# First expert products: all high halves of the weights of a unit before all low halves, and another pacing of the weight splits

## Chip, core and metric

The kernel runs on one core of one Trainium2 chip. The metric is device time in microseconds (us) for one execution of the whole layer; lower is better. The time before the change is the median of three runs, 2164.36 us (2163.01 to 2168.81 us).

## What is computed

The program is one decoder layer for 1024 tokens of width 1024: a projection, two kinds of attention, an output projection, then a mixture of 32 experts of which each token uses four. Only the experts matter for this change. In the reference (cut; the router and the sorting of tokens are left out):

```python
def expert_block(args):
    xe, e = args
    gu = xe @ w_gate_up[e] + b_gate_up[e]            # 1024 -> 2048
    g = jnp.minimum(gu[:, :D_FF], SWIGLU_LIMIT)
    u = jnp.clip(gu[:, D_FF:], -SWIGLU_LIMIT, SWIGLU_LIMIT)
    act = (u + 1.0) * (g * jax.nn.sigmoid(SWIGLU_ALPHA * g))
    return act @ w_down[e] + b_down[e]               # 1024 -> 1024
```

Everything is float32, and the 32 experts have 3 x 4 MB of weights each that must be read from HBM once.

## The kernel before

The experts run one after the other, the largest and the smaller ones alternating. An expert has a fixed number of token columns C (`CAPS`: 200 down to 136 for 17 of them, with the first, and 128 down to 96 for 15).

**Chunks.** The weights of an expert arrive as twelve chunks of 1 MB, `[128, 4, 512]` in float32: eight of the first matrix (buffers `eraw`, five of them) and four of the second (`draw`, four). SP issues their DMAs (line 782).

**Splits.** A chunk of the first matrix is split in two halves (`split_half`): ScalarE writes the high part of half a chunk as fp32r into a buffer `hb` (line 796, twelve buffers of half a chunk each), and VectorE subtracts it and writes the remainder, the low part, as bf16 into `ha` (line 797, six buffers of a whole chunk). A chunk of the second matrix is used as it is.

**Units.** The first matrix is worked in four units of 512 output columns: gate, up, gate, up (`first_products`, called twice in each pass of the loop over `half`). A unit takes two chunks (the two halves `kh` of the 1024 rows that are summed over) and four PSUM banks, one for each 128 output columns `j`. For each of its 8 row blocks `k` and 4 values of `j` there are two products on TensorE: a high one (line 1167: weights `hb`, moving data `xx`, which holds the tokens' high and low parts, 2C columns and at least 256) and a low one (line 1171: weights `ha` in bf16, moving data `xb`, the tokens in bf16, C columns). That is 32 high and 32 low products. The two kinds alternate in runs: 16 high, 16 low (first chunk), then 8 high, 8 low for `j` = 0, 1 and 8 high, 8 low for `j` = 2, 3 (second chunk). Below, H16 is a run of 16 high products, L8 a run of 8 low ones, and so on.

**After a unit.** ScalarE adds the bias while it reads a bank (`tb`, line 1179), VectorE adds the other columns of the bank (line 1183 for gate, 1181 for up), and they make the activation `aa` (lines 1197, 1198, 1207, 1208). Then 64 products with the second matrix follow (line 1220, in float32; the trace has two records for each), their results go to `yT` (line 1225), and in the middle of them stand the transposes of the next expert's tokens (`stage_t`, lines 1146 to 1150). The transposes of the result (line 1237, at most 16), the weighting (line 1239, `y`) and the scatter are put off (`later(1, back)`) until the next expert has done its first chunk; they stand on TensorE between L16 and H8 of its first unit.

**Order and pacing.** From the experts on, the order on TensorE, ScalarE, VectorE and SP is the order in which the code calls them. After each chunk `done(c)` drops the chunk from `at_["open"]`, the number of half chunks that are split and not yet used (at most 12), and calls `pump(n)`, which issues the loads for which a buffer is free and up to n splits: 1 after a chunk of the first matrix, 2 after one of the second. So `open` is 12, 10, 8 and 6 at the starts of the four units, 4 after them, and 12 again after the second matrix.

Of the kernel before, what the change touches and what calls it, by code (L numbers as in the profile page):

```python
# [20 lines left out]
P = 128  # L21
# [3 lines left out]
KT = D // P  # L25
# [52 lines left out]
def hybrid_layer(ctx: ExitStack, tc: tile.TileContext, x, c_t, w_ada, b_ada_t, b_ada, norm1_t, w_in,  # L78
                 qk_g, lam_in, diff_g, w_out, norm2_g, w_router, b_router, w_gate_up, b_gate_up,
                 w_down, b_down, b_exp_t, out):  # L80
    nc = tc.nc
# [102 lines left out]
    with ExitStack() as st:  # L184
# [335 lines left out]
        with ExitStack() as so:  # L520
# [241 lines left out]
            parts, reg = {}, {0: 0}  # L762
            at_ = {"dma": 0, "split": 0, "use": 0, "open": 0}
            raws, held = {}, {"eraw": 0, "draw": 0}
# [7 lines left out]
            def kind_of(d):  # L772
                return "eraw" if d % NCH < NGU else "draw"

            def load_chunk():
                d, kind = at_["dma"], kind_of(at_["dma"])
                i, w, n, kh = CHUNKS[d]
                e = expert_of(i)
                if d % NCH == LIX and 0 < i < E - 1:
                    lists(i + 1)  # L780
                raws[d] = pools[kind][0].tile([P, 4, NC_], F32, name=kind, bufs=pools[kind][1])
                nc.sync.dma_start(raws[d], w[ds(e, 1), kh * 512:(kh + 1) * 512, n * NC_:(n + 1) * NC_]
                                  .rearrange("o (k p) n -> p (o k) n", p=P))
                held[kind] += 1
                at_["dma"] += 1

            def split_half():

                t = at_["split"]
                c, q = t // 16 * NCH + t % 16 // 2, t % 2  # L790
                raw = raws[c][:, 2 * q:2 * q + 2]
                h_ = slot(False).rearrange("p (k n) -> p k n", k=2)
                if q == 0:
                    parts[c] = [], slot(True).bitcast(BF16).rearrange("p (k n) -> p k n", k=4)
                l_ = parts[c][1][:, 2 * q:2 * q + 2]
                nc.scalar.activation(h_, raw, AF.Copy)  # L796
                nc.vector.tensor_tensor(l_, raw, h_.bitcast(F32), OP.subtract)  # L797
                parts[c][0].extend((h_[:, j], l_[:, j]) for j in range(2))
                if q:
                    raws.pop(c)  # L800
                    held["eraw"] -= 1
                at_["open"] += 1
                at_["split"] += 1

            def pump(more):

                limit = min(at_["split"] + more, E * 16)
                while True:
                    d, t = at_["dma"], at_["split"]
                    kind = kind_of(d)  # L810
                    if d < len(CHUNKS) and kind in pools and held[kind] < pools[kind][1]:
                        load_chunk()
                    elif t < limit and t // 16 * NCH + t % 16 // 2 < d and at_["open"] < NH:
                        split_half()
                    else:
                        return
# [248 lines left out]
    with ExitStack() as se:  # L1065
# [23 lines left out]
        def take():  # L1089

            c = at_["use"]
            at_["use"] += 1
            return c, parts[c][0] if kind_of(c) == "eraw" else raws[c]

        def bank():
            return ps4.tile([P, 512], F32, name="gu", bufs=8)

        todo = []

        def done(c):  # L1100

            if kind_of(c) == "eraw":
                parts.pop(c)
                at_["open"] -= 2
                pump(1)
            else:
                raws.pop(c)
                held["draw"] -= 1
                pump(2)
            for t in todo:  # L1110
                t[0] -= 1
            while todo and todo[0][0] <= 0:
                todo.pop(0)[1]()
# [38 lines left out]
        def scatter(y, sl, n):  # L1152
            nc.gpsimd.indirect_dma_start(  # L1153
                out=out, out_offset=bass.IndirectOffsetOnAxis(ap=sl.bitcast(I32)[:n, 0:1], axis=0),
                in_=y[:n], in_offset=None, compute_op=OP.add)

        def first_products(st):


            C, xx, xb = st["C"], st["xk"], st["xb"]  # L1160
            pg = [bank() for _ in range(4)]
            for kh in range(2):
                c, w = take()
                for js in ((0, 1), (2, 3)) if kh else ((0, 1, 2, 3),):
                    for j in js:
                        for k in range(4):
                            nc.tensor.matmul(pg[j][:, :max(256, 2 * C)], w[k][0][:, j * P:(j + 1) * P], xx[4 * kh + k],  # L1167
                                             start=(kh + k == 0), stop=False)
                    for j in js:
                        for k in range(4):  # L1170
                            nc.tensor.matmul(pg[j][:, C:2 * C], w[k][1][:, j * P:(j + 1) * P], xb[:, 4 * kh + k],  # L1171
                                             start=False, stop=(kh == 1 and k == 3))
                if kh == 0:
                    done(c)
            return c, pg

        def joined(dst, p, C, bias, more=0.0):
            t = ap_.tile([P, C], F32, name="tb", bufs=TB)
# [6 lines left out]
        def expert(st, between):  # L1185
            C, bc = st["C"], st["bc"]
            a = ap_.tile([P, KT, C], F32, name="aa")
            for half in range(2):
                c, pg = first_products(st)
                gts = []  # L1190
                for q in range(2):
                    gt = ap_.tile([P, 2, C], F32, name="gt", bufs=2)
                    for j in range(2):
                        f = 4 * half + 2 * q + j
                        joined(gt[:, j], pg[2 * q + j], C, bc[:, f:f + 1])
                    sg = ap_.tile([P, 2, C], F32, name="sg")
                    nc.scalar.activation(sg, gt, AF.Sigmoid, scale=1.702)  # L1197
                    nc.vector.tensor_mul(gt, gt, sg)  # L1198
                    gts.append(gt)
                done(c)  # L1200
                c, pg = first_products(st)
                for q in range(2):
                    ut = ap_.tile([P, 2, C], F32, name="ut")
                    f = 4 * half + 2 * q
                    for j in range(2):
                        joined(ut[:, j], pg[2 * q + j], C, bc[:, KT + f + j:KT + f + j + 1], 1.0)
                    nc.vector.tensor_scalar(ut, ut, 8.0, -6.0, op0=OP.min, op1=OP.max)
                    nc.vector.scalar_tensor_tensor(a[:, f:f + 2], gts[q], GATE7, ut, op0=OP.min, op1=OP.mult)
                done(c)


            pg = [bank() for _ in range(4)]
            yT = ap_.tile([P, KT, C], F32, name="yT")
            for kh in range(2):
                for n in range(2):
                    c, w = take()
                    for j in range(4):
                        p = pg[2 * n + j // 2][:, j % 2 * 256:j % 2 * 256 + C]
                        for k in range(4):
                            nc.tensor.matmul(p, w[:, k, j * P:(j + 1) * P], a[:, 4 * kh + k],  # L1220
                                             start=(kh + k + j % 2 == 0), stop=(kh == 1 and k == 3 and j % 2 == 1))
                    if kh:
                        for j in range(4):
                            f = 4 * n + j
                            nc.scalar.activation(yT[:, f], pg[2 * n + j // 2][:, j % 2 * 256:j % 2 * 256 + C], AF.Identity,  # L1225
                                                 bias=bc[:, 2 * KT + f:2 * KT + f + 1], scale=1.0)
                    done(c)
                if kh == 0:
                    between()

            def back():
                for (t0, n), sl in zip(st["blocks"], st["slots"]):
                    y = ap_.tile([P, D], F32, name="y", bufs=2)
                    for g in range(2):
                        py = bank()
                        for k in range(4):
                            nc.tensor.transpose(py[:n, k * P:(k + 1) * P], yT[:, 4 * g + k, t0:t0 + n], ident)
                        cs = slice(g * 512, (g + 1) * 512)
                        nc.vector.scalar_tensor_tensor(y[:n, cs], py[:n], sl[:n, 1:2], gate2[:n, cs],  # L1239
                                                       op0=OP.mult, op1=OP.mult)  # L1240
                    scatter(y, sl, n)
            later(1, back)
# [57 lines left out]
        st = stage_g(0)  # L1300
# [7 lines left out]
        for i in range(E):  # L1308
            nxt = stage_g(i + 1) if i + 1 < E else None
            expert(st, lambda: nxt and stage_t(nxt))  # L1310
            st = nxt
# [4 lines left out]
    with ExitStack() as sf:  # L1316
# [4 lines left out]
        with tc.For_i(0, n_over, 1) as i:  # L1321
# [44 lines left out]
            for n in range(2):  # L1366
                c = slice(n * 512, (n + 1) * 512)
# [52 lines left out]
```

## Time and profile before

| | us |
|---|---|
| median of 3 runs | 2164.36 (2163.01 to 2168.81) |
| the profiled execution | 2167.32 |
| its span in the trace | 2165.5 |
| busy in it: TensorE (PE) | 2094.8 (97%) |
| VectorE (DVE) | 1499.6 (69%) |
| ScalarE (ACT) | 1150.2 (53%) |
| experts: from the first product to the last piece of the last expert | 742.8 to about 2153 |

The profile is of one execution. An engine is busy while at least one of its instructions runs; matmuls are pipelined (the recorded duration of one is longer than the distance to the next), so for TensorE the distances between the starts of runs are read, not the durations. A timeline row has the start, the length, the engine, the source line, the names (out<-in), the shape and the count of equal instructions that follow each other. A row of waits has the engine and line that waited, for whom, the total in us, how often, and the longest.

### The profile page before, as it was taken

Reading aid. Unit: us, or ns where it says so; the run is one execution under the profiler, and the core shown is the slowest. Engines: PE = TensorE matmul, PEld = TensorE weight load, DVE = VectorE, ACT = ScalarE, POOL = GpSimd, SP = SyncE. Lnnn points to the kernel's source line nnn. Section 1 sums busy time; section 2 is a strip of 40 time slices with the busy share of each in tenths; the row PEclk is TensorE's granted clock in tenths of the full one; section 3 lists DMA queues with packets and bytes.
Section 4 is the critical chain, followed back from the end, with each engine's and each line's share of the span. In section 5 each row is a group of like instructions: output and inputs, shape, how many; then the busy total and the mean of one; then the engine's idle time right before and its main releaser. Section 6 shows DMA issues by size and latency. Waiting matters only on the chain. (4 is left out here: it accounts for less than half of the span.)

```text
span 2165.5 us, 43655 instructions
## 1 busy us (share of the span) xinstructions
PE 2094.8 (97%) x16922; PEld 1957.5 (90%) x16922; DVE 1499.6 (69%) x2946; ACT 1150.2 (53%) x2263; POOL 429.3 (20%) x444
## 2 busy tenths in 40 slices
PE   7999999999999699999999999999999999999997
PEld 6877778998777699999999999999999999999997
DVE  6587756776666876677667677776767767667763
ACT  3522224777633455566456565656556656656652
POOL 2255532111045401111011111110111101101100
PEclk9999999999999799999999999999999999999999
DMA  7267886442224598799799999989989989999882
GB/s 294 73 163 215 221 230 172 114 109 76 89 105 153 192 356 299 247 334 350 255 292 326 300 314 319 332 312 343 315 297 312 361 297 320 323 315 335 297 320 60
DMA packets 272404, 548.98 MB, mean 254 GB/s; under 512 B 30675, under 2 KB 30691, under 8 KB 272067
## 3 DMA queue, kind: packets, MB, share of 16 engines
q1 hardware_dynamic: 250323, 490.09, 65.4%
q0 software_dynamic: 21872, 56.08, 11.1%
q8 instruction: 134, 2.20, 0.4%
q14 instruction: 75, 0.61, 0.1%
HBM read 501.31 MB, written 44.77 MB: 252 GB/s over the span
## 5 line engine op out<-in xcount | busy, mean ns | idle before, releaser
L797 DVE TENSOR_TENSOR ha<-eraw,hb 128x1024 bf16<-128x1024 f32 x512 | 601.3, 1224 | 233.5 <-ACT hb L796 233.0
L1167 PE MATMUL gu<-xx,hb 128*128 128x256 f32 (+13 forms) x4096 | 641.5, 304 | 0.6 <-DVE xx L1149 0.6
L1167 PEld LDWEIGHTS gu<-xx,hb 128*128 128x128 f32 x4096 | 561.1, 190 | 1.0 <-DVE xx L1149 0.8
L796 ACT ACTIVATE hb<-eraw 128x1024 fp32r<-128x1024 f32 x512 | 506.7, 1053 | 34.1 <-DMA eraw<-in_w_gate_up_dram 34.0
L1220 PE MATMUL gu<-aa,draw 128*128 128x128 f32 (+19 forms) x4096 | 521.2, 288 | 0.0
L1220 PEld LDWEIGHTS gu<-aa,draw 128*128 128x128 f32 x4096 | 511.2, 191 | 0.6
L1171 PE MATMUL gu<-xb,ha 128*128 128x128 bf16 (+19 forms) x4096 | 316.2, 224 | 0.0
L1179 ACT ACTIVATE tb<-gu,bcol 128x128 f32<-128x128 f32 (+19 forms) x512 | 164.6, 371 | 253.8 <-PE gu L1171 225.7
L1171 PEld LDWEIGHTS <-ha 128*128 128x128 bf16 x4096 | 246.6, 98 | 28.4 <-issue 3.3
L1153 POOL DMA_INDIRECT out_dram<-y,slot x47 | 81.6, 1736 | 528.3 <-DVE y L1239 251.4
L1126 POOL DMA_INDIRECT xg<-h2d,slot x47 | 54.5, 1160 | 629.0 <-PE gu L1146 381.8
L1225 ACT ACTIVATE yT<-gu,bcol 128x128 f32<-128x128 f32 (+19 forms) x256 | 82.4, 374 | 126.6 <-PE gu L1220 126.5
L572 DVE CUSTOM_DVE_ANT_0 p<-pss,bias 128x1024 f32<-128x1024 f32 (+7 forms) x128 | 94.4, 755 | 49.5 <-ACT p L581 22.2
L606 PE MATMUL po<-vsb,pT 128*128 128x64 f32 (+1 forms) x864 | 111.1, 275 | 2.6 <-ACT pT L600 1.5
L606 PEld LDWEIGHTS po<-vsb,pT 128*128 128x128 f32 x864 | 105.6, 194 | 4.8 <-ACT pT L600 1.8
L581 ACT ACTIVATE p<-p,mn 128x1024 f32<-128x1024 f32 (+7 forms) x128 | 98.6, 773 | 12.8 <-DVE mn L572 12.1
L1197 ACT ACTIVATE sg<-gt 128x256 f32<-128x256 f32 (+19 forms) x128 | 55.8, 436 | 89.2 <-DVE gt L1183 89.2
L461 PE MATMUL pp<-wh,hb 128*128 128x512 f32 x240 | 101.7, 424 | 0.0
L1198 DVE TENSOR_TENSOR gt<-gt,sg 128x256 f32<-128x256 f32 (+19 forms) x128 | 57.4, 448 | 63.4 <-ACT sg L1197 63.4
L112 POOL TENSOR_TENSOR rrs<-vrs,nhalf 128x8 f32<-128x8 f32 (+2 forms) x48 | 66.6, 1386 | 165.3 <-DVE vrs L110 160.2
L463 PE MATMUL pp<-wl,hb 128*128 128x512 f32 x240 | 94.9, 395 | 0.0
L462 PE MATMUL pp<-wh,hb 128*128 128x512 f32 x240 | 94.8, 395 | 0.0
(265 smaller groups left out, 2623.6 us busy)
## 6 DMA issues: line engine op xcount, KB each, us to landing
eraw<-in_w_gate_up_dram SPq DMA_DIRECT2D x256, 1024.0 KB
draw<-in_w_down_dram SPq DMA_DIRECT2D x128, 1024.0 KB
wraw<-in_w_ada_dram SPq DMA_DIRECT2D x32, 512.0 KB
wraw<-in_w_in_dram SPq DMA_DIRECT2D x23, 512.0 KB
hb<-in_w_ada_dram SPq DMA_DIRECT2D x16, 512.0 KB
qd<-tt POOLq DMA_DIRECT2D x32, 256.0 KB, 4.0
kd<-tt POOLq DMA_DIRECT2D x32, 256.0 KB, 4.2
ha<-qd SPq DMA_DIRECT2D x32, 256.0 KB
```

Of the source, the lines that this page charges most:

```text
L461: nc.tensor.matmul(pp, hh[b][:, k], wh[:, kk], start=(k == 0), stop=False)
L462: nc.tensor.matmul(pp, hl[b][:, k], wh[:, kk], start=False, stop=False)
L463: nc.tensor.matmul(pp, hh[b][:, k], wl[:, kk], start=False, stop=(k == KT - 1))
L572: nc.vector.tensor_tensor_reduce(p[:, :n], pss[:, :n], bias[:, (NB - 1 - ib) * P:(NB - 1 - ib) * P + n], -1.0, 3.0e38, OP.add, OP.min, mn)
L581: nc.scalar.activation(p, p, AF.Exp, bias=self.mn[c], scale=-1.0, accum_out=self.l[:, c:c + 1])
L606: nc.tensor.matmul(self.po[:, :w], self.pT[:, k], vsb[self.br][:, k, self.h * w:(self.h + 1) * w], start=(k == 0), stop=(k == self.ib))
L796: nc.scalar.activation(h_, raw, AF.Copy)
L797: nc.vector.tensor_tensor(l_, raw, h_.bitcast(F32), OP.subtract)
L1167: nc.tensor.matmul(pg[j][:, :max(256, 2 * C)], w[k][0][:, j * P:(j + 1) * P], xx[4 * kh + k], start=(kh + k == 0), stop=False)
L1171: nc.tensor.matmul(pg[j][:, C:2 * C], w[k][1][:, j * P:(j + 1) * P], xb[:, 4 * kh + k], start=False, stop=(kh == 1 and k == 3))
L1179: nc.scalar.activation(t, p[:, C:2 * C], AF.Identity, bias=bias, scale=1.0)
L1220: nc.tensor.matmul(p, w[:, k, j * P:(j + 1) * P], a[:, 4 * kh + k], start=(kh + k + j % 2 == 0), stop=(kh == 1 and k == 3 and j % 2 == 1))
```

## The change

In a unit both chunks are taken at its start. The high products of the first chunk come first (H16), then those of the second (H16), then all 32 low products, bank by bank (L32: 8 for each `j`). Each product stays as it was; the number of instructions on every engine is the same. The first chunk is no longer handed back alone: between the two H16 stands `step()`, a `pump(1)` and the countdown of `todo` (so the result's transposes of the previous expert now stand between the two H16 of the first unit), and both chunks are handed back at the unit's end, with two splits after a gate unit and one after an up unit. After the chunks of the second matrix come 2, 1, 2 and 1 splits in place of 2, 2, 2 and 2. `open` is then 11, 10, 8 and 7 at the starts of the units (12, 11, 9 and 8 after the `step()` in them), 5 after them and 11 again after the second matrix.

```diff
--- before.py
+++ after.py
@@ -1097,16 +1097,19 @@
 
         todo = []
 
-        def done(c):
-
-            if kind_of(c) == "eraw":
-                parts.pop(c)
-                at_["open"] -= 2
-                pump(1)
-            else:
-                raws.pop(c)
-                held["draw"] -= 1
-                pump(2)
+        def done(*cs, more=1):
+
+            for c in cs:
+                if kind_of(c) == "eraw":
+                    parts.pop(c)
+                    at_["open"] -= 2
+                else:
+                    raws.pop(c)
+                    held["draw"] -= 1
+            step(more)
+
+        def step(more=1):
+            pump(more)
             for t in todo:
                 t[0] -= 1
             while todo and todo[0][0] <= 0:
@@ -1159,20 +1162,19 @@
 
             C, xx, xb = st["C"], st["xk"], st["xb"]
             pg = [bank() for _ in range(4)]
+            two = [take() for _ in range(2)]
+            w = two[0][1] + two[1][1]
             for kh in range(2):
-                c, w = take()
-                for js in ((0, 1), (2, 3)) if kh else ((0, 1, 2, 3),):
-                    for j in js:
-                        for k in range(4):
-                            nc.tensor.matmul(pg[j][:, :max(256, 2 * C)], w[k][0][:, j * P:(j + 1) * P], xx[4 * kh + k],
-                                             start=(kh + k == 0), stop=False)
-                    for j in js:
-                        for k in range(4):
-                            nc.tensor.matmul(pg[j][:, C:2 * C], w[k][1][:, j * P:(j + 1) * P], xb[:, 4 * kh + k],
-                                             start=False, stop=(kh == 1 and k == 3))
+                for j in range(4):
+                    for k in range(4 * kh, 4 * kh + 4):
+                        nc.tensor.matmul(pg[j][:, :max(256, 2 * C)], w[k][0][:, j * P:(j + 1) * P], xx[k],
+                                         start=(k == 0), stop=False)
                 if kh == 0:
-                    done(c)
-            return c, pg
+                    step()
+            for j in range(4):
+                for k in range(KT):
+                    nc.tensor.matmul(pg[j][:, C:2 * C], w[k][1][:, j * P:(j + 1) * P], xb[:, k], start=False, stop=(k == KT - 1))
+            return two[0][0], two[1][0], pg
 
         def joined(dst, p, C, bias, more=0.0):
             t = ap_.tile([P, C], F32, name="tb", bufs=TB)
@@ -1186,7 +1188,7 @@
             C, bc = st["C"], st["bc"]
             a = ap_.tile([P, KT, C], F32, name="aa")
             for half in range(2):
-                c, pg = first_products(st)
+                c, c_, pg = first_products(st)
                 gts = []
                 for q in range(2):
                     gt = ap_.tile([P, 2, C], F32, name="gt", bufs=2)
@@ -1197,8 +1199,8 @@
                     nc.scalar.activation(sg, gt, AF.Sigmoid, scale=1.702)
                     nc.vector.tensor_mul(gt, gt, sg)
                     gts.append(gt)
-                done(c)
-                c, pg = first_products(st)
+                done(c, c_, more=2)
+                c, c_, pg = first_products(st)
                 for q in range(2):
                     ut = ap_.tile([P, 2, C], F32, name="ut")
                     f = 4 * half + 2 * q
@@ -1206,7 +1208,7 @@
                         joined(ut[:, j], pg[2 * q + j], C, bc[:, KT + f + j:KT + f + j + 1], 1.0)
                     nc.vector.tensor_scalar(ut, ut, 8.0, -6.0, op0=OP.min, op1=OP.max)
                     nc.vector.scalar_tensor_tensor(a[:, f:f + 2], gts[q], GATE7, ut, op0=OP.min, op1=OP.mult)
-                done(c)
+                done(c, c_)
 
 
             pg = [bank() for _ in range(4)]
@@ -1224,7 +1226,7 @@
                             f = 4 * n + j
                             nc.scalar.activation(yT[:, f], pg[2 * n + j // 2][:, j % 2 * 256:j % 2 * 256 + C], AF.Identity,
                                                  bias=bc[:, 2 * KT + f:2 * KT + f + 1], scale=1.0)
-                    done(c)
+                    done(c, more=2 - n)
                 if kh == 0:
                     between()
 
```

TensorE, in an expert of 120 columns, its first unit and the start of its second (`hb`, `ha`: high and low weights; `yT`: the previous expert's result, turned). Before:

```order
L1167 MATMUL gu<-xx,hb 128x256 x16
L1171 LDWEIGHTS ha
L1171 MATMUL gu<-xb,ha 128x120
...
L1237 MATMUL gu<-ident,yT 128x128 x8
L1237 MATMUL gu<-ident,yT 44x128 x8
L1167 MATMUL gu<-xx,hb 128x256 x8
...
L1167 MATMUL gu<-xx,hb 128x256 x8
...
L1167 MATMUL gu<-xx,hb 128x256 x16
```

and of the changed kernel:

```order
L1170 MATMUL gu<-xx,hb 128x256 x16
L1239 MATMUL gu<-ident,yT 128x128 x8
L1239 MATMUL gu<-ident,yT 44x128 x8
L1170 MATMUL gu<-xx,hb 128x256 x16
L1176 LDWEIGHTS ha
L1176 MATMUL gu<-xb,ha 128x120
...
L1170 MATMUL gu<-xx,hb 128x256 x32
```

The low products, each a weight load and a matmul, stood behind every run of high ones (16, 8 and 8 times the pair); now 32 pairs stand behind 32 high products, and the transposes stand inside the high ones. In the second to fourth unit nothing interrupts H32.

ScalarE, the same expert, from the end of the previous expert's second matrix to the second gate unit (`hb<-eraw`: splits; `tb`, `sg`: a unit's evaluation). Before:

```order
L1225 ACTIVATE yT<-gu,bcol 128x172 x4
L796 ACTIVATE hb<-eraw 128x1024 x3
L1179 ACTIVATE tb<-gu,bcol 128x120 x2
L1197 ACTIVATE sg<-gt 128x240
L1179 ACTIVATE tb<-gu,bcol 128x120 x2
L1197 ACTIVATE sg<-gt 128x240
L796 ACTIVATE hb<-eraw 128x1024 x2
L1179 ACTIVATE tb<-gu,bcol 128x120 x4
L796 ACTIVATE hb<-eraw 128x1024 x2
```

and of the changed kernel:

```order
L1227 ACTIVATE yT<-gu,bcol 128x172 x4
L796 ACTIVATE hb<-eraw 128x1024 x2
L1181 ACTIVATE tb<-gu,bcol 128x120 x2
L1199 ACTIVATE sg<-gt 128x240
L1181 ACTIVATE tb<-gu,bcol 128x120 x2
L1199 ACTIVATE sg<-gt 128x240
L796 ACTIVATE hb<-eraw 128x1024 x3
L1181 ACTIVATE tb<-gu,bcol 128x120 x4
L796 ACTIVATE hb<-eraw 128x1024 x2
```

Between the evaluation of a gate unit and that of the up unit behind it stand three splits in place of two, and before a gate unit of a new expert two in place of three; VectorE's order has the same shift with `ha<-eraw,hb`.

## Rows read from the trace of the kernel before

**Rows 1.** Busy time of the engines, from the page: us, share, instructions.

```profile
PE 2094.8 (97%) x16922; PEld 1957.5 (90%) x16922; DVE 1499.6 (69%) x2946; ACT 1150.2 (53%) x2263; POOL 429.3 (20%) x444
```

**Rows 2.** TensorE's waits from 742.8 us to the end.

```profile
PE gu L1167 <- DVE xx L1149: 0.6, 1, 0.6
```

**Rows 3.** Busy time by window: length, PE, PEld, DVE, ACT, POOL, clock, DMA share, GB/s.

```profile
742.80:2153.00 1410.20, 1409.76 (x13056) 1376.13 (x13056) 983.85 (x1626) 814.45 (x1499) 185.13 (x202) 1.00 0.90 307
1075.00:1380.00 305.00, 305.00 (x2904) 298.25 (x2903) 218.95 (x355) 181.10 (x335) 45.87 (x46) 1.00 0.96 313
```

**Rows 4.** Timeline of TensorE, 120 columns: a whole unit, then a later start.

```profile
1516.93 2.14 PE L1167 MATMUL gu<-xx,hb 128*128 128x256 f32 x16
1518.91 1.01 PE L1171 MATMUL gu<-xb,ha 128*128 128x120 bf16 x16
1519.73 1.19 PE L1167 MATMUL gu<-xx,hb 128*128 128x256 f32 x8
1520.77 0.59 PE L1171 MATMUL gu<-xb,ha 128*128 128x120 bf16 x8
1521.17 1.19 PE L1167 MATMUL gu<-xx,hb 128*128 128x256 f32 x8
...
1522.61 2.14 PE L1167 MATMUL gu<-xx,hb 128*128 128x256 f32 x16
...
1528.30 2.14 PE L1167 MATMUL gu<-xx,hb 128*128 128x256 f32 x16
```

**Rows 5.** Timeline of TensorE, 172 columns: high runs of one unit.

```profile
1383.92 2.75 PE L1167 MATMUL gu<-xx,hb 128*128 128x344 f32 x16
...
1387.68 1.50 PE L1167 MATMUL gu<-xx,hb 128*128 128x344 f32 x8
...
1389.59 1.51 PE L1167 MATMUL gu<-xx,hb 128*128 128x344 f32 x8
...
1391.51 2.75 PE L1167 MATMUL gu<-xx,hb 128*128 128x344 f32 x16
```

**Rows 6.** Timeline of TensorE, 200 columns: starts of runs in one unit.

```profile
848.43 3.17 PE L1167 MATMUL gu<-xx,hb 128*128 128x400 f32 x16
851.44 1.55 PE L1171 MATMUL gu<-xb,ha 128*128 128x200 bf16 x16
852.76 1.71 PE L1167 MATMUL gu<-xx,hb 128*128 128x400 f32 x8
...
854.95 1.70 PE L1167 MATMUL gu<-xx,hb 128*128 128x400 f32 x8
...
857.13 3.17 PE L1167 MATMUL gu<-xx,hb 128*128 128x400 f32 x16
```

**Rows 7.** Timeline of TensorE, first unit of an expert of 120 columns.

```profile
1428.99 1.92 PE L1237 MATMUL gu<-ident,yT 128*128 128x128 f32 x16
1430.67 1.20 PE L1167 MATMUL gu<-xx,hb 128*128 128x256 f32 x8
1431.71 0.59 PE L1171 MATMUL gu<-xb,ha 128*128 128x120 bf16 x8
```

**Rows 8.** Groups from 742.8 to 2153 us: busy, mean ns, idle before.

```profile
L797 DVE TENSOR_TENSOR ha<-eraw,hb 128x1024 bf16<-128x1024 f32 x508 | 596.7, 1224 | 233.5 <-ACT hb L796 233.0 <-issue 0.5
L796 ACT ACTIVATE hb<-eraw 128x1024 fp32r<-128x1024 f32 x508 | 502.8, 1054 | 34.1 <-DMA eraw<-in_w_gate_up_dram 34.0
L1171 PEld LDWEIGHTS <-ha 128*128 128x128 bf16 x4096 | 246.6, 98 | 28.4 <-issue 3.3
```

**Rows 9.** Timeline of VectorE, 120 columns: splits, then the end of an up unit.

```profile
1520.64 2.36 DVE L797 TENSOR_TENSOR ha<-eraw,hb 128x1024 bf16<-128x1024 f32 x2 [0.54 <-ACT hb L796]
...
1525.07 0.41 DVE L1208 SCALAR_TENSOR_TENSOR aa<-gt,ut 128x240 f32<-128x240 f32 x1
```

**Rows 10.** ScalarE's waits for chunks, from 900 us on.

```profile
ACT hb L796 <- DMA eraw<-in_w_gate_up_dram: 31.8, 8, 7.4
```

**Rows 11.** The DMA queue's own waits (SP), from 850 us on.

```profile
SPq L782 <- DVE ha L797: 626.9, 159, 10.5
```

## The prediction

> **What bounds the kernel now.** I read the page's busy times first: TensorE is busy in 2094.8 us of the span [rows 1], far more than any other engine. Then its waits over the expert stage: 0.6 us in all, at the first product of the first expert [rows 2]. The window over that stage says the same: 1409.76 us busy of 1410.20, at a granted clock of 1.00, which is the full 2.4 GHz [rows 3]. So for 1410 us the time is the sum of the distances between the starts of TensorE's instructions; nothing it needs comes late. VectorE (984 us) and ScalarE (814 us) have slack in the same window, and the DMA engines are 0.90 busy. What the change does to TensorE's own stream counts directly; what it does to the others counts only where it makes TensorE wait.
>
> The third view is TensorE's timeline of a whole unit at 120 columns [rows 4], read by starts. H16 with L16 takes 1519.73 - 1516.93 = 2.80 us. A pair H8, L8 does half that work; the two pairs behind take 1521.17 - 1519.73 = 1.44 and 1522.61 - 1521.17 = 1.44 us. Half of 2.80 is 1.40. If the products alone made the time, two short pairs would last as long as the long one; they last 2.88 against 2.80, so one more pair of runs costs 0.08 us. Each pair changes the kind of product twice, high to low and back to high, and the rows can't be explained by a new chunk, since the second H8 begins with a chunk already in use and its pair is no shorter than the first. The same reading at 172 columns gives 1.91 + 1.92 - 3.76 = 0.07 [rows 5], at 200 columns 2.19 + 2.18 - 4.33 = 0.04 us [rows 6]. I call this the price of a change: 0.08 at the narrow widths, on average 0.055 at the wide ones.
>
> **The change part by part.** No instruction is added or taken away; the edits are an order and a pacing.
>
> First, the order of a unit. The second to fourth unit of an expert go from three pairs of runs to one: two changes less each, six in an expert. In the first unit the transposes of the last expert's result cut the high run, H16, transposes, H16, L32. A high run that begins behind transposes pays as much as one behind low products: H8 behind them lasts 1431.71 - 1430.67 = 1.04 us [rows 7], and H8 behind L16 lasts 1520.77 - 1519.73 = 1.04 us too [rows 4]. So this unit still has two entries into high products (its start, and behind the transposes) where it had three, and saves one change. That is seven for an expert, and eight for the first one, which has no transposes inside. Wide experts, 17 with the first: 17 x 7 + 1 = 120 changes at 0.055 us, 6.6 us. Narrow ones: 15 x 7 = 105 at 0.08 us, 8.4 us. Sum: 15.0 us.
>
> What the rows do not show is the step from a high product to a transpose, which is new (31 times). Its nearest rows are the prices of a change: from nothing to 0.08 us, so 0 to 2.5 us of loss. Nor do they exclude that the first unit saves its second change as well, 2.5 us of gain. I take neither. For the price itself the ends are 0.04 and 0.08 everywhere: 225 x 0.04 = 9.0 and 225 x 0.08 = 18.0 us. With the two unknowns on top the gain lies between 6.5 and 20.5 us.
>
> Do runs of 32 go on as runs of 16 do? In the long pair the low run takes 1519.73 - 1518.91 = 0.82 us for 16 products, 51 ns each; L8 takes 1521.17 - 1520.77 = 0.40 us, 50 ns each [rows 4]. Doubling the run did not slow it. I take 51 ns for the products 17 to 32 as well; the other end is the first rival.
>
> Second, the splits. They are spaced 16 to an expert as before, and I cost the new pacing at nothing. What hides it is the stock of halves that are already split. At the start of the fourth unit there were 6 and are now 7, of which that unit uses 4; the last of the four was issued at the end of the second unit, before as now. That is a whole unit ahead (5.68 us at 120 columns, [rows 4]), and a split lasts 1.05 us on ScalarE and 1.22 us on VectorE [rows 8]. The second chunk's high halves are now wanted behind H16 instead of H16 and L16, 0.82 us sooner; the lows of both later. No new wait for a buffer arises: the stock reaches 12 halves, in six chunks, only at the `step()` of a first unit, which is what the twelve `hb` and six `ha` hold.
>
> Third, the queue behind the splits. Between the evaluation of a gate unit and that of the up unit there are now three splits on VectorE, not two, and the up unit's reads of its banks stand behind them: 1.22 us later. At 120 columns that evaluation ended at 1525.07 + 0.41 = 1525.48 us, and the fourth unit, which takes these banks, began at 1528.30 [rows 4, 9]: 2.82 us of cover. Off it go 1.22 us and two savings of 0.16 us, and 1.3 us stay. If that cover went, TensorE would wait once for each such place, up to 32 times. The banks also become complete closer together, in the last four runs of 8 low products; the evaluation of a gate unit starts a little later, with the same cover behind it. The transposes of the result come 0.82 us sooner behind the second matrix and have one split less ahead of them on both engines.
>
> Fourth, the loads. SP's largest wait is for VectorE, that is for a free buffer, 626.9 us in 159 waits [rows 11]. So the loads follow the splits, and with the same splits in an expert they keep their place. SP issues the same loads in the same order (only the reading of the overflow count moves, nine loads back), and GpSimd's gathers and scatters stand in the same order too.
>
> So the sum is 15.0 us, all of it on the path. The profiled execution took 2167.32 us, 3 us over the median; against it the sum gives 2152.3, against the median 2164.4 - 15.0 = 2149.4 us.
>
> **The rivals.** *The low runs get too long.* Each low product needs its own weights, a load of 98 ns [rows 8], and the products follow each other at 51 ns: that works only while loads run ahead. If the lead is used up after 16 pairs, products 17 to 32 of a unit, 128 x 16 = 2048 in all, come at 98 ns: 47 ns more each at 120 columns, 96 us if all were so narrow; at 200 columns the distance is already (852.76 - 851.44) / 16 = 82 ns [rows 6], so 16 ns more, 33 us. The middle, 64 us, against a gain of 15: 2213 us. It decides from 15.0 / 2048 = 7 ns a product. Against it: no slowing between 8 and 16. The page "TensorE: Matmul & The Clock Gate" of the Trainium skill (section "Back-to-back issue gap") speaks for it: it gives about 81 ns for a sustained stream of weight loads and matmuls of 128 columns, against 56 ns for one matmul by itself. By that the late products would lose 25 ns each, an estimate of 51 us from this page's figures; runs of 16 in this trace don't agree with it, and no run here is longer. Chance 0.06.
>
> *The weights come too late.* ScalarE waited eight times for a chunk, 31.8 us in all and up to 7.4 us [rows 10], and between 1075 and 1380 us the DMA engines were 0.96 busy [rows 3]. A faster TensorE asks for the same bytes sooner. If that stretch is held to its transfers, its 7 experts lose their share of the gain, 7/32 x 15.0 = 3.3 us: 2152.7 us. If all of the stage is, nothing is left: 2164.4 us. Against it: the waits of 7.4 us never reached TensorE, and over the whole stage 0.90 would only become 0.91. Chance of a loss over 5 us: 0.08.
>
> *The change of kind is not what costs.* The price may hang on something that stays, such as the number of bank changes or the signals to ScalarE; the order would then move nothing: 2164.4 us. Two independent widths besides 120 columns show the price, so 0.05.
>
> **How the numbers follow.** My forecast has 0.80, the three rivals 0.06, 0.08 and 0.05, and 0.01 is left for something else. A measurement here can tell about 0.3% from no change, 6.5 us, so faster means under 2157.9 us. The forecast's own range, 2143.9 to 2157.9 us, lies there whole; of the late weights half does. That makes faster 0.80 + 0.04 + 0.01 = 0.85, the same 0.04 + 0.05 = 0.09, slower 0.06. The range reaches from 2144 to 2160 us, which takes in the mild half of the second rival.
>
> **What would show it.** In the changed profile a unit of 120 columns should last about 5.68 - 0.16 = 5.52 us from start to start, its H32 about 3.9 and its L32 about 1.65 us, the last 8 low products as close as the first 8. TensorE's waits should stay near 0.6 us, and its busy time should fall by the whole gain. Low products that drift apart behind the sixteenth prove the first rival; waits of TensorE for `hb`, `ha` or a bank, with ScalarE's waits for chunks grown, the second; a unit of 5.68 us the third. I am wrong if the gain comes with new waits, or if the unit shrinks and the time doesn't.

## The result, and the profile after

The changed kernel takes 2152.31 us (median of 5 runs, 2151.51 to 2153.65), the kernel before 2167.80 us on the same occasion (5 runs, 2163.01 to 2170.88). The medians are 15.5 us apart. The ratio is 0.9931 with a 95% interval of 0.9916 to 0.9945: a gain of 15.0 us, between 11.9 and 18.2. Of all executions told of here one was slow, of the kernel order_only below (4026.11 us, at a mean granted clock of 0.91 where the others had 0.99), and its ratio leaves it out. The two extra runs of the kernel before lie higher than the three known at the forecast, so its median is 3.4 us higher than the one I started from; that is why 2152.3 is reached and not 2149.4.

TensorE's waits over the experts, in the profile after, the same kind of row as in [rows 2]:

```profile
PE gu L1170 <- DVE xx L1152: 0.6, 1, 0.6
```

Nothing new makes it wait. Its window ends earlier, and the DMA engines are 0.91 busy in place of 0.90 [rows 3]:

```profile
742.80:2139.50 1396.70, 1395.95 (x13056) 1380.99 (x13056) 977.52 (x1627) 824.80 (x1499) 182.62 (x203) 1.00 0.91 310
```

The window over the stage was 1410.2 us long and is 1396.7, and TensorE's own busy time in it fell by 13.8 us, from 1409.76 to 1395.95: the whole difference is there. The timeline after, of an expert of 120 columns from its start to the second matrix (compare [rows 4, 7]):

```profile
1503.27 2.15 PE L1170 MATMUL gu<-xx,hb 128*128 128x256 f32 x16
1505.26 1.91 PE L1239 MATMUL gu<-ident,yT 128*128 128x128 f32 x16
1506.92 2.14 PE L1170 MATMUL gu<-xx,hb 128*128 128x256 f32 x16
1508.91 1.85 PE L1176 MATMUL gu<-xb,ha 128*128 128x120 bf16 x32
1510.57 4.04 PE L1170 MATMUL gu<-xx,hb 128*128 128x256 f32 x32
1514.45 1.85 PE L1176 MATMUL gu<-xb,ha 128*128 128x120 bf16 x32
1516.12 4.03 PE L1170 MATMUL gu<-xx,hb 128*128 128x256 f32 x32
1519.99 1.85 PE L1176 MATMUL gu<-xb,ha 128*128 128x120 bf16 x32
1521.66 4.03 PE L1170 MATMUL gu<-xx,hb 128*128 128x256 f32 x32
1525.53 1.85 PE L1176 MATMUL gu<-xb,ha 128*128 128x120 bf16 x32
1527.22 3.00 PE L1222 MATMUL gu<-aa,draw 128*128 128x120 f32 x25
```

A unit lasts 1516.12 - 1510.57 = 5.55 us (forecast 5.52, before 5.68), its H32 3.88 and its L32 1.67 us. L32 is 52 ns a product, as L16 was 51: the longer run does not slow down. At 172 and at 200 columns:

```profile
1378.78 5.30 PE L1170 MATMUL gu<-xx,hb 128*128 128x344 f32 x32
1383.93 2.58 PE L1176 MATMUL gu<-xb,ha 128*128 128x172 bf16 x32
1386.30 5.31 PE L1170 MATMUL gu<-xx,hb 128*128 128x344 f32 x32
...
848.43 6.10 PE L1170 MATMUL gu<-xx,hb 128*128 128x400 f32 x32
854.37 2.92 PE L1176 MATMUL gu<-xb,ha 128*128 128x200 bf16 x32
857.07 1.16 PE L1170 MATMUL gu<-xx,hb 128*128 128x400 f32 x5
```

A unit takes 7.52 and 8.64 us, before 7.59 [rows 5] and 8.70 us [rows 6].

### The profile page after: what moved, and what is told of

Its sections match the earlier page's. It is cut to its first block, busy times and chain, and to the rows that moved or that the text cites. A ratio compares the mean times of both kernels' runs of the same rounds, so it can differ in the third digit from the quotient of the medians.

```text
span 2151.8 us, 43624 instructions
## 1 busy us (share of the span) xinstructions
PE 2079.3 (97%) x16922; PEld 1960.2 (91%) x16922; DVE 1493.2 (69%) x2946; ACT 1160.6 (54%) x2263; POOL 427.0 (20%) x444
## 5 line engine op out<-in xcount | busy, mean ns | idle before, releaser
L1170 PE MATMUL gu<-xx,hb 128*128 128x256 f32 (+13 forms) x4096 | 588.0, 300 | 0.6 <-DVE xx L1152 0.6
L1170 PEld LDWEIGHTS gu<-xx,hb 128*128 128x128 f32 x4096 | 554.6, 190 | 1.0 <-DVE xx L1152 0.8
L1181 ACT ACTIVATE tb<-gu,bcol 128x128 f32<-128x128 f32 (+19 forms) x512 | 177.0, 372 | 256.7 <-PE gu L1176 188.3
L1176 PE MATMUL gu<-xb,ha 128*128 128x128 bf16 (+19 forms) x4096 | 271.6, 224 | 0.0
L1151 ACT ACTIVATE xx<-gu 128x512 fp32r<-128x512 f32 (+19 forms) x98 | 39.5, 475 | 110.6 <-PE gu L1149 110.4
L1185 DVE TENSOR_TENSOR gt<-gu,tb 128x128 f32<-128x128 f32 (+19 forms) x256 | 68.5, 296 | 39.8 <-ACT tb L1181 35.7
```

The costliest lines, as they stand in the source:

```text
L1181: nc.scalar.activation(t, p[:, C:2 * C], AF.Identity, bias=bias, scale=1.0)
```

## The experiments

My theory: the whole gain is the 225 changes of kind that are gone, at a fixed price each, and the pacing is worth nothing. The rivals: a part of the gain is the pacing's; or the price is not of the change of kind. Each kernel was timed against the kernel before on the same chip, in five rounds.

**order_only**, the changed kernel with the old amounts of splits:

```diff
-                done(c, c_, more=2)
+                done(c, c_)
...
-                    done(c, more=2 - n)
+                    done(c, more=2)
```

> TensorE's order is that of the changed kernel; the splits are paced as in the kernel before (one at each of the two hand-backs of a unit, two after each chunk of the second matrix), so the stock is 11, 9, 7 and 5 halves at the starts of the units and 3 after them. Theory (the gain is 225 changes of kind less, the pacing is worth nothing): 13 to 17 us faster than the kernel before, a unit of 120 columns 5.53 us, TensorE's waits 0.6 us. Rival (the new pacing is needed for the gain): TensorE waits for a split or a bank in the third or fourth units, and at least 5 us of the gain are missing.

Measured: 2152.24 against 2167.28 us, ratio 0.9933 (0.9920 to 0.9946), 15.0 us between the medians. TensorE waited 0.6 us, though the stock was only 5 halves at the start of the fourth unit, and a unit of 120 columns took 1431.93 - 1426.40 = 5.53 us:

```profile
1426.40 4.02 PE L1170 MATMUL gu<-xx,hb 128*128 128x256 f32 x32
1430.27 1.85 PE L1176 MATMUL gu<-xb,ha 128*128 128x120 bf16 x32
1431.93 4.03 PE L1170 MATMUL gu<-xx,hb 128*128 128x256 f32 x32
```

The order alone brings all of it.

**pacing_only**, the changed kernel with the runs of before:

```diff
-                for j in range(4):
-                    for k in range(4 * kh, 4 * kh + 4):
-                        (a high product)
+                for js in ((0, 1), (2, 3)) if kh else ((0, 1, 2, 3),):
+                    for j in js:
+                        for k in range(4 * kh, 4 * kh + 4):
+                            (a high product)
+                    for j in js:
+                        for k in range(4 * kh, 4 * kh + 4):
+                            (a low product)
                 if kh == 0:
                     step()
-            (all low products)
```

> Both chunks of a unit are handed back together and the splits are paced as in the changed kernel, but the products stand in the runs of before (16, 16, 8, 8, 8, 8). Theory (the gain is the order's alone): within 3 us of the kernel before, a unit of 120 columns 5.67 us. Rival (a part of the gain is the pacing's): faster than before by 5 us or more.

Measured: 2167.60 against 2167.28 us, ratio 1.0004 (0.9995 to 1.0012). The pacing neither gains nor costs. Summed over the starts of all units in the trace, the experts take 0.02 us more than before.

**runs_of_4** and **runs_of_1**, the kernel before with more changes:

```diff
-                for js in ((0, 1), (2, 3)) if kh else ((0, 1, 2, 3),):
+                for js in ((0,), (1,), (2,), (3,)):
```

and for runs of 1 both products in one loop over `j` and `k`.

> The kernel before with shorter runs: 4 high and 4 low products for each bank in each chunk, eight pairs of runs in a unit in place of three, 5 x 128 = 640 more changes of kind; everything else as before. Theory (each change costs 0.04 to 0.08 us, however long the runs are): 26 to 51 us slower, nearest to 640 x 0.067 = 43 us, and no new waits of TensorE. Rival (the price hangs on the end of a bank's run or on a signal, not on the change of kind): within 10 us of before. Second rival (the price grows as the runs shrink, since weight loads can be pulled ahead less): over 60 us slower.

> The kernel before with one high and one low product by turns: 32 pairs in a unit in place of three, 29 x 128 = 3712 more changes. Theory (a fixed price of 0.067 us for a change): 3712 x 0.067 = 249 us slower, 150 to 300. Rival (the price sits in the second high product of a run, which comes 200 ns behind the first; a run of one has no second): much less than 150 us slower. Second rival (a weight load that can't be pulled ahead at all, 190 ns for a high one and 98 ns for a low one): over 350 us slower.

Measured: 2207.64 against 2167.28 us, ratio 1.0188 (1.0175 to 1.0201): 40.4 us for 640 changes, 0.063 us each. And 2412.27 against 2167.28 us, 1.1132 (1.1118 to 1.1147): 245.0 us for 3712 changes, 0.066 us each. The price is about the same whether a run has 16, 8, 4 products or one (0.061 us in the traces for the changes that the order takes away), and TensorE waited 0.6 us in both. The timeline of runs_of_1 at 120 columns:

```profile
1664.84 0.36 PE L1166 MATMUL gu<-xx,hb 128*128 128x256 f32 x1
1665.05 0.23 PE L1168 MATMUL gu<-xb,ha 128*128 128x120 bf16 x1
1665.09 0.36 PE L1166 MATMUL gu<-xx,hb 128*128 128x256 f32 x1
1665.29 0.23 PE L1168 MATMUL gu<-xb,ha 128*128 128x120 bf16 x1
1665.33 0.36 PE L1166 MATMUL gu<-xx,hb 128*128 128x256 f32 x1
```

A pair takes (1665.33 - 1664.84) / 2 = 0.245 us, where a high and a low product inside long runs take 3.88 / 32 + 1.67 / 32 = 0.173 us. The recorded start of the high product is only 0.04 us behind the low one; the low one behind it starts 0.21 us later. So the lost time stands between the start of the high product and what follows it, which asks for its cause.

**cover_16** and **cover_96.** In the kernel before, the weight loads (PEld) around a return to high products stand like this:

```profile
1518.90 0.85 PEld L1171 LDWEIGHTS <-ha 128*128 128x128 bf16 x16
1519.71 1.01 PEld L1167 LDWEIGHTS gu<-xx,hb 128*128 128x128 f32 x8
```

The last low product alone, the second high load alone, and the high loads of the whole stage (times, mean ns):

```profile
1519.70 0.22 PE L1171 MATMUL gu<-xb,ha 128*128 128x120 bf16 x1
...
1519.82 0.19 PEld L1167 LDWEIGHTS gu<-xx,hb 128*128 128x128 f32 x1
...
L1167 PEld LDWEIGHTS gu<-xx,hb 128*128 128x128 f32 x4096 | 561.1, 190 | 1.0 <-DVE xx L1149 0.8
```

The first load of high weights begins at 1519.71 us, just behind the start of the last low product at 1519.70. One high load lasts 190 ns, a low one 98 ns [rows 8]. Theory: the price is that part of this load that the one product before it doesn't hide. Not all of the 190 ns can count, since 190 - 52 = 138 ns would be about twice the price; the second high load begins only 0.11 us behind the first. Then an extra, useless low product in front of the high run stands under the load, whatever its width:

```diff
+                    if (js[0] == 0 and kh) or (kh == 0 and u):
+                        nc.tensor.matmul(pg[3][:, 400:416], w[3][1][:, js[-1] * P:(js[-1] + 1) * P],
+                                         xb[:, 4 * kh + 3, :16], start=False, stop=False)
```

> The kernel before with 224 extra low products, one behind the last low product of a run wherever a high run of the same unit follows (not behind the first chunk of an expert's first unit): the same weights again, 16 columns, into an unused part of a bank. Theory (the price of going back to high products is the load of the high weights, 190 ns long, which begins with the last low product and is hidden only while that product runs): the extra product stands under the load, so each costs what the low product before it takes, 43 to 86 ns with 61 in the mean, 224 x 0.061 = 13.7 us, the same as with 96 columns. Rival (a fixed price behind the end of the low products): each costs its own distance, some 28 ns, 6 us.

> As cover_16 with 96 columns in each extra low product. Theory (the load of the high weights hides it): 13.7 us slower than before, within 2.5 us of cover_16. Rival (a fixed price): each costs 43 ns, 9.6 us, and the difference to cover_16 is 224 x (96 - 16) / 2.4 ns = 7.5 us less what a product takes at least, 4 to 7.5 us.

Measured: 2180.02 against 2166.01 us, ratio 1.0065 (1.0053 to 1.0077), 14.0 us; and 2181.62 against 2166.01 us, 1.0070 (1.0057 to 1.0083), 15.6 us. The intervals overlap. Summed over the starts of the units, the experts take 14.15 and 14.21 us more than before: the six times wider product costs 0.06 us more in all 224 places together. What an extra product costs goes with the low products before it: by the same sums 52 ns in the narrow experts, where low products are 52 ns apart, and 70 ns in the wide ones, where they are 69 ns apart. One place of each kernel, at 168 columns (extra product: L1174), first 16 columns, then 96:

```profile
1563.05 0.75 PE L1171 MATMUL gu<-xb,ha 128*128 128x168 bf16 x8
1563.64 0.17 PE L1174 MATMUL gu<-xb,ha 128*128 128x16 bf16 x1
1563.67 1.47 PE L1167 MATMUL gu<-xx,hb 128*128 128x336 f32 x8
1564.98 0.76 PE L1171 MATMUL gu<-xb,ha 128*128 128x168 bf16 x8
```

```profile
1566.63 0.75 PE L1171 MATMUL gu<-xb,ha 128*128 128x168 bf16 x8
1567.22 0.21 PE L1174 MATMUL gu<-xb,ha 128*128 128x96 bf16 x1
1567.24 1.47 PE L1167 MATMUL gu<-xx,hb 128*128 128x336 f32 x8
1568.56 0.76 PE L1171 MATMUL gu<-xb,ha 128*128 128x168 bf16 x8
```

From the start of the extra product to the next low run it is 1.34 us in both. The rival, a fixed price behind the end of the low products, falls: it wanted 4 to 7.5 us between the two kernels. The extra product brings a load of its own low weights; that this load is what it costs doesn't fit either, since it lasts 98 ns at every width.

**tails_between**, an attempt to use this. Transposes are 109 ns apart in the trace and hide more of the load than a low product. The result's transposes of the last expert are cut into groups of four, and most groups are put where a low run ends:

```diff
+                if tail:
+                    tail.pop(0)()
                 done(c, c_, more=2)
...
+                if tail and half == 0:
+                    tail.pop(0)()
                 done(c, c_)
```

It ran beside the changed kernel itself, as **after_again**.

> The changed kernel with the result's transposes of the last expert not in one block inside the first unit, but four at a time: with two token blocks one group there and one behind each of the first three units, with one block one group behind each of the first two. So 16 x 3 + 15 x 2 = 78 of the 96 returns from low to high products go over transposes, which are 109 ns apart. Theory (the load of the high weights is hidden by the product before it): such a return costs next to nothing, 78 x (0.060 us less 0.01 to 0.02) = 3 to 4 us less than the changed kernel, 2147.5 to 2149.5 us, if TensorE waits for no bank. Rival (a group takes a bank more between two units, so the fourth bank of the next unit is one that the unit before it has only just filled): TensorE waits at the fourth bank, and the time is the changed kernel's or longer.

> The changed kernel itself once more, beside tails_between on the same chip: 0.9931 of the kernel before (0.9916 to 0.9945).

Measured: 2150.08 us (2145.74 to 2153.68), ratio 0.9921 (0.9907 to 0.9935) against 2167.52 us; the changed kernel 2151.91 us, 0.9931 (0.9917 to 0.9944). The median is 1.8 us under that of the changed kernel and misses the expected 2147.5 to 2149.5, and the two intervals overlap, so the times don't separate them. The traces do: TensorE waits 0.6 us in all, and the sum over the starts is 3.5 us shorter than in the changed kernel beside it, as expected. A return over transposes, at 120 columns:

```profile
1426.67 1.85 PE L1178 MATMUL gu<-xb,ha 128*128 128x120 bf16 x32
1428.36 0.60 PE L1242 MATMUL gu<-ident,yT 128*44 128x128 f32 x4
1428.71 4.03 PE L1170 MATMUL gu<-xx,hb 128*128 128x256 f32 x32
1432.59 1.85 PE L1178 MATMUL gu<-xb,ha 128*128 128x120 bf16 x32
1434.28 0.60 PE L1242 MATMUL gu<-ident,yT 128*44 128x128 f32 x4
```

The unit with four transposes lasts 1434.28 - 1428.36 = 5.92 us, 0.37 more than one of the changed kernel without any; four transposes by themselves are 4 x 109 = 436 ns. Its median is the lowest measured; that it is faster than the changed kernel is shown by its trace and not by its times.

## Why the prediction was right

**The bound.** Right: the time follows TensorE's stream, with waits of 0.6 us before and after.

**The price of a change.** The step is right and its sizes a little high. Summed over the starts of the second to fourth units in both traces, a change less saved 0.071 us in the 15 narrow experts (taken: 0.08) and 0.051 us in the 17 wide ones (0.055); together 11.7 us for 192 changes, where the forecast had 7.2 + 5.6 = 12.8 us (90 of the narrow and 102 of the wide kind). Starts that are rounded to 0.01 us, in differences of three, do not give more than this.

**The first unit.** Counted as one change less, 0.055 and 0.08 us; it saved 0.069 and 0.102 us on average, 2.6 us in 31 experts where the forecast had 2.1. The step that was new, from a high product to a transpose, costs nothing: the 16 products before the transposes take 1505.26 - 1503.27 = 1.99 us, as H16 did before low ones (1.98, [rows 4]). What the unit saves beyond one return is two further steps from high to low products, 13 ns each by the starts of single products in the trace before, and in the narrow experts some 12 ns for the step from low products to a transpose.

One reading behind this count was wrong: that a high run behind transposes pays as much as one behind low products. Both H8 last 1.04 us, but the first distance in them holds the time of the instruction before, 109 ns for a transpose and 52 for a low product. Behind the transposes next to nothing was lost, as tails_between showed. The count of one change came out right all the same, since the entry that went away in the first unit is one behind low products.

**The sum.** The first unit of the first expert took 0.44 us longer in this trace, where the granted clock had the lower of its levels for longer (0.65 of full in the mean from 745 to 751 us, 0.77 in the trace before); the sum in the traces is then 13.9 us, and 11.7 + 2.6 = 14.3 us without that unit, against 15.0 forecast and 15.0 measured by the ratio. That forecast and ratio agree to a tenth is partly luck: the price was taken 1.1 us too high, the first units 0.5 us too low, and the interval is 6 us wide.

**Splits, queue and loads at nothing.** Right, and shown by pacing_only and order_only. The cover behind the third split was mis-sized in the safe direction: I had 2.82 us fall to 1.3. In the profile after, the up unit's evaluation stands so:

```profile
1513.32 3.50 DVE L797 TENSOR_TENSOR ha<-eraw,hb 128x1024 bf16<-128x1024 f32 x3 [0.54 <-ACT hb L796]
...
1518.89 0.41 DVE L1210 SCALAR_TENSOR_TENSOR aa<-gt,ut 128x240 f32<-128x240 f32 x1
```

It ends at 1519.30 us and the fourth unit begins at 1521.66: 2.36 us are left. Three splits now start 2.75 us behind the start of that unit (1510.57), where two started 3.71 us behind it [rows 4, 9]; the result's transposes and the weighting behind them are done earlier, so that the gate unit's evaluation is too.

**Rivals.** *Low runs too long*: false. L32 runs at 52 ns at 120 columns. At 128 columns:

```profile
1078.65 1.96 PE L1176 MATMUL gu<-xb,ha 128*128 128x128 bf16 x32
1080.42 1.79 PE L1170 MATMUL gu<-xx,hb 128*128 128x256 f32 x13
```

that is 1.77 / 32 = 55 ns. The pace of about 81 ns that the page "TensorE: Matmul & The Clock Gate" of the Trainium skill gives (section "Back-to-back issue gap") for a sustained stream of loads and matmuls of 128 columns does not hold for 32 such pairs in this trace; the measurement decides. *Weights too late*: ScalarE's waits for chunks,

```profile
ACT hb L796 <- DMA eraw<-in_w_gate_up_dram: 27.1, 7, 6.8
```

did not grow (31.8 us before, [rows 10]), and none reached TensorE. *Not the change of kind*: false by runs_of_4 and runs_of_1.

## What to carry to other kernels

Where one engine is busy all the time, read the distances between the starts of its runs: runs of two lengths with the same work give the price of a change between them by subtraction. Here it paid to let the products with the longer weight loads stand in long runs; and where a return to them couldn't be avoided, a longer instruction in front of it (a transpose, 109 ns, in place of a low product, 52 ns at 120 columns) hid nearly all of the load. With a unit's work already split in advance, the pacing of the splits was free in both orders.

## What the runs showed of the hardware

The price of a return is not a toll behind the low products: it is what is left of a time that runs from the start of the last one. At 120 columns a low product lasts 52 ns and a change costs (5.68 - 5.55) / 2 = 65 ns by these two units; at 200 columns it lasts 2.70 / 32 = 84 ns and a change costs (8.70 - 8.64) / 2 = 30 ns. Such a change is a step to low products and a return to high ones. The starts of single products in the trace of the kernel before take the two apart. From the start of the last low product to that of the second high one pass 112 ns more than one distance between high products, in the mean of 310 returns (those of the first expert left out), and between 110 and 114 ns in the mean of each of the 20 widths. A low product covers its own distance of that, so a return costs 60 ns at 120 columns and 26 ns at 200. The step from high to low adds some 13 ns at every width. Together they are 8 to 9 ns more than the price by units above, which this reading leaves open. From an extra product of 16 or of 96 columns on the time is 110 ns, and from the last transpose on it is 112 ns too, of which the transpose covers 109. So it is the same behind bf16 products and behind float32 transposes.

At all 321 returns of that trace the first high load begins 1 or 2 ns behind the start of the last low product, and the next one 110 ns behind the first in the median. The page "TensorE: Matmul & The Clock Gate" (Trainium skill, section "Step-by-step: what each phase is for") says that the next tile's weights load while the running one is multiplied; this trace agrees, and it shows that this load was hidden by one product only. That the 112 ns are the load, and not something else that begins with it, is argued from these starts and was not tested by itself; why the load doesn't begin earlier was not tried.
